# A delta-rule inverse with its first off-diagonal products written ahead of the diagonal blocks' copies, and filler steps dealt anew

## The chip, the cores and the metric

The kernel runs on one core of a Trainium2 chip. The metric is the device time of one execution in microseconds (us). The engines are PE (TensorE), DVE (VectorE), ACT (ScalarE), POOL (GpSimd) and SP (SyncE, which issues most DMAs).

## What is computed

Two layers (DEPTH = 2) work on 512 latent tokens and 256 context tokens of width 1024. Each layer has one input projection for three head groups, whose outputs are concatenated and projected again:

```python
h_l, h_c = rglru_bidir(a_l, a_c, ...)                 # gated linear recurrence, two directions
nb_l = neighbourhood_attend(q, k, v, kb_c, vb_c, rpb) # 6 heads, windows on an 8 x 64 grid
o_l, o_c = gdn_bidir(...)                             # gated delta rule, 4 heads, chunks of 64
y_l = concatenate([h_l * silu(za), nb_l * silu(zn), gdn_output(o_l, nw, zg)], -1) @ w_out
x_new = layer_norm(ALPHA * x + gate * y_l, ln_g, ln_b)
```

The change is in the third group. For each chunk of 64 tokens the delta rule solves a unit lower triangular system:

```python
a_mat = where(strict, einsum('nbhid,nbhjd->nbhij', kb, kc) * decay, 0.0) + eye(64)
u = triangular_solve(a_mat, vc * beta, lower=True, unit_diagonal=True)
w = triangular_solve(a_mat, kb * exp(gcum), lower=True, unit_diagonal=True)
```

There are 12 chunks (8 latent, 4 context), 4 heads and 2 directions. The kernel inverts each 64 x 64 matrix as two 32 x 32 diagonal blocks and one off-diagonal block, which is a product of three 32 x 32 matrices.

## The kernel before, in words

In each layer a generator `gdn()` gives the delta rule in 48 steps, and a generator `fill()` gives the rest: the attention's projections (`na_proj`, matmuls `pj<-uh,wh` and the like at L489, 24 for an output block of 512 or 256 columns), its scores and outputs (`na_att`), and the recurrence. A loop takes one step of `gdn()`, then as many steps of `fill()` as the table `CFG["n"][l]` says for that step, and calls a modulation gate at the steps of `CFG["mods"][l]`. The steps are: gates 0 and 1, chunk sets `cs` 2 to 7, transposes `t` 8 to 13, the decay products `w8` 14 to 19, two steps `lnT` 20 and 21, ten elimination steps `k3` to `k30` 22 to 31, `tz` 32, the inverse 33 to 35, and 12 scan steps from 36. A scheduler then sets the order on each engine, from this order of writing and from priorities; each engine's queue is run in order. `together` gives matmuls a high priority behind the first of them.

The parts that matter, for one layer:

- The matrices of the chunks lie in `bm`. Its diagonal blocks go into `dgc`, in a layout in which one partition row is one element of the block: two copies on ACT (L738) and two on DVE (L740), each 32 partitions by 1536. DVE transposes `dgc` to `ln` (L744).
- Elimination on DVE: 30 pairs of a product into `tmp` (L750) and a sum into `ln` (L752).
- DVE transposes `ln` into `tz` (L758, L759), the left factors of the off-diagonal products. It then transposes `ln` in place for d = 0 and d = 1, the two directions (L763), and ACT copies the blocks back into `bm`, four copies of 32 x 768 for each d (L767). The d = 0 copies read `ln` with a stride.
- Then two groups follow one another. Each has 48 products `gab<-tz,bm` (L779), an ACT copy to `zs` (L781), 48 products `gab<-bm,zs` (L788) and four DVE copies into `bm` (L794). All use the two banks of `gab`, one for the first products and one for the second.
- The scan's first ACT copies are `sb<-vtm` (L835). `dgc`, `ln`, `tz`, `so` and `sb` share two buffers (tag "g8"), so `sb` takes the buffer that `ln` had.

The attention's tiles that the profile names are `kT` and `qT` (ACT L924, DVE L925), `vT` (ACT L922), its transposes `nT` (PE L932) and their copies `vt` (ACT L933), scores `nS`, exponentials `nsb` (L980), `ptb` (L986), the product `nT<-ptb,vt` (PE L198, where the helper `mm` stands), and a weight's high and low part `wh` (ACT L237) and `wl` (DVE L238).

Of the kernel before, what the change touches and what calls it, by code (L numbers as in the profile page):

```python
# [5 lines left out]
F32 = mybir.dt.float32  # L6
# [50 lines left out]
ZXB = 5  # L57
CFG = {"gp": 3000, "sp": 2000, "mixP": 0.5, "wo": 1, "ye": 2, "rgord": [[0, 1, 0, 0, 0, 1, 0, 2, 1, 1, 2, 2, 2, 1, 2], [0, 0, 1, 0, 1, 0, 0, 2, 1, 1, 2, 1, 2, 2, 2]], "n": [[0, 0, 0, 0, 0, 0, 0, 0, 0, 2, 0, 3, 0, 0, 0, 0, 1, 2, 2, 0, 0, 1, 1, 0, 1, 0, 2, 0, 2, 0, 0, 0, 1, 0, 0, 0, 1, 1, 2, 0, 0, 2, 1, 0, 4, 0, 0, 0], [0, 0, 0, 0, 0, 0, 0, 0, 0, 1, 0, 0, 1, 0, 0, 0, 1, 2, 0, 1, 3, 0, 0, 1, 2, 0, 2, 0, 0, 0, 0, 0, 1, 0, 0, 2, 0, 0, 0, 3, 0, 0, 0, 0, 1, 0, 2, 2]], "mods": [[3, 5, 6, 8, 10, 11], [2, 11]]}

# [80 lines left out]
def _build(tc, I, out, dbg=None):  # L140
# [22 lines left out]
    def ps(tag, shape=(128, 512), dt=F32):  # L163
        return pp.tile(list(shape), dt, name=tag, tag=tag, bufs=PB[tag])
# [32 lines left out]
    def mm(o, a, b, start, stop):  # L197
        return lambda: T.matmul(o, a, b, start=start, stop=stop)  # L198
# [271 lines left out]
    for l in range(DEPTH):  # L470
# [99 lines left out]
        def gdn():  # L570
# [190 lines left out]
            yield  # L761
            for d in range(2):
                V.transpose(out=lview(d), in_=lview(d))  # L763
                for q in range(4):
                    c0 = 32 * (q % 2)
                    pr = slice(32 * q, 32 * q + 32)
                    S.activation(bm[pr, 24 * d:24 * d + 24, c0:c0 + 32],  # L767
                                 lview(d)[pr, :, 0:24].rearrange("p i m -> p m i"), AF.Copy)
            yield
            for mg_ in range(2):  # L770
                m0 = 12 * mg_
                zs = gp.tile([128, 512], F32, name="zs2", tag="qk", bufs=3)[:, 0:384].rearrange("p (m j) -> p m j", j=32)
# [167 lines left out]
        def na_att(hp):  # L940
            qT, kT, vt, z = nas[hp]
            for part in range(1 if last else 2):
                nq = 4 if part == 0 else 2
                nk = 4 if part == 0 else 2
                mx = np_.tile([128, 3, 4, 2], F32, name="mx", tag="mx", bufs=2)
                for b in range(nq):
                    p_ = ps("nS", TWO)
                    q0 = 128 * b + (0 if part == 0 else 512)
                    if part == 0 and b != 2:
                        sl = nbl[0] % 2  # L950
                        nbl[0] += 1
                        dma(out=bt[:, 2 * sl:2 * sl + 2], in_=I["rpb"][l, 2 * hp:2 * hp + 2, NA_KIND[b]].rearrange("h p k -> p h k"))
                    todo = []
                    for i, (a, c) in enumerate(((0, 0), (0, 1), (1, 0))):
                        for h2 in range(2):
# [14 lines left out]
                    for h2 in range(2):  # L970
# [12 lines left out]
                        for g in range(nk):  # L983
# [282 lines left out]
```

## Time and profile before

| | us |
|---|---|
| three runs | 893.71, 895.1, 898.94 |
| median | 895.1 |
| profiled execution | 896.31 |
| its span | 894.5 |
| PE busy in the span | 830.9 |
| DVE busy | 673.5 |
| ACT busy | 460.4 |
| POOL busy | 28.5 |

The span goes from the first to the last instruction of the profiled execution. The mean granted clock of PE over the span is 0.981 of full speed.

### The profile page before, as it was taken

Reading aid. Unit: us, or ns where it says so; the run is one execution under the profiler, and the core shown is the slowest. Engines: PE = TensorE matmul, PEld = TensorE weight load, DVE = VectorE, ACT = ScalarE, POOL = GpSimd, SP = SyncE. Lnnn points to the kernel's source line nnn. Section 1 sums busy time; section 2 is a strip of 40 time slices with the busy share of each in tenths; the row PEclk is TensorE's granted clock in tenths of the full one; section 3 lists DMA queues with packets and bytes.
Section 4 is the critical chain, followed back from the end, with each engine's and each line's share of the span. In section 5 each row is a group of like instructions: output and inputs, shape, how many; then the busy total and the mean of one; then the engine's idle time right before and its main releaser. Section 6 shows DMA issues by size and latency. Waiting matters only on the chain.

```text
span 894.5 us, 17977 instructions
## 1 busy us (share of the span) xinstructions
PE 830.9 (93%) x7164; PEld 634.6 (71%) x7164; DVE 673.5 (75%) x1524; ACT 460.4 (51%) x842; POOL 28.5 (3%) x101
## 2 busy tenths in 40 slices
PE   5999999998997999999999999999899699999885
PEld 3677777776776777877778778776777567776674
DVE  3458565897994699669969656998899467878867
ACT  3354443446457244489817634445554735349812
POOL 0000000000000011100001000000000000020001
PEclk8999999999999999999999999999899899999998
DMA  8826732211112010236533262121122121131433
GB/s 318 327 77 220 265 132 99 60 48 43 54 53 66 26 37 3 101 128 200 181 117 138 94 225 72 48 71 41 52 76 69 39 60 51 49 119 59 158 133 122
DMA packets 44900, 94.58 MB, mean 106 GB/s; under 512 B 5248, under 2 KB 10240, under 8 KB 44816
## 3 DMA queue, kind: packets, MB, share of 16 engines
q1 hardware_dynamic: 44816, 93.43, 31.2%
q8 instruction: 56, 0.92, 0.4%
q14 instruction: 28, 0.23, 0.1%
HBM read 84.22 MB, written 9.19 MB: 104 GB/s over the span
## 4 chain that ended last, share of the span: by engine, by line
PE 49%; DVE 26%; ACT 14%; issue 7%; DMA 3%; POOL 1%; SPq 1%; DVEq 0%; POOLq 0%; ACTq 0%
PE pj L489 23%; PE pj L1207 3%; DVE nsb L976 2%; DVE wl L238 2%; PE nT L984 2%; ACT bm L767 2%; DVE ln L752 2%; DVE tmp L750 2%; PE x L853 1%; PE x L1207 1%; PE nT L198 1%; PE x L198 1%; DVE ti L1085 1%; PE nS L590 1%; ACT wh L237 1%
## 5 line engine op out<-in xcount | busy, mean ns | idle before, releaser
L489 PE MATMUL pj<-uh,wh 128*128 128x512 f32 (+1 forms) x680 | 245.8, 362 | 0.8 <-ACT vT L922 0.8
L489 PE MATMUL pj<-uh,wl 128*128 128x512 f32 (+1 forms) x680 | 241.9, 356 | 0.0
L489 PE MATMUL pj<-ul,wh 128*128 128x512 f32 (+1 forms) x680 | 241.8, 356 | 0.0
L489 PEld LDWEIGHTS pj<-uh,wh 128*128 128x128 f32 x680 | 129.8, 191 | 22.7 <-issue 6.2
L489 PEld LDWEIGHTS pj<-ul,wh 128*128 128x128 f32 x680 | 129.7, 191 | 16.1 <-issue 2.5
L489 PEld LDWEIGHTS pj<-uh,wl 128*128 128x128 f32 x680 | 129.6, 191 | 16.0 <-issue 2.5
L238 DVE TENSOR_TENSOR wl<-raw,wh 128x512 fp32r<-128x512 f32 (+1 forms) x106 | 72.0, 681 | 48.6 <-ACT wh L237 47.1
L237 ACT ACTIVATE wh<-raw 128x512 fp32r<-128x512 f32 (+1 forms) x106 | 65.6, 622 | 63.8 <-PE pj L489 59.7
L980 ACT ACTIVATE nsb<-nsb,mx 128x512 f32<-128x512 f32 x48 | 34.5, 720 | 36.2 <-DVE mx L978 35.9
L986 ACT ACTIVATE ptb<-nT 128x512 f32<-128x512 f32 (+1 forms) x60 | 33.4, 556 | 23.8 <-PE nT L984 23.2
L984 PE MATMUL nT<-cst,nsb 128*128 128x128 f32 x216 | 36.8, 284 | 2.2 <-DVE mx L978 1.0
L543 DVE SCALAR_TENSOR_TENSOR cs<-xp,tph,cs 128x771 f32<-128x771 f32 (+1 forms) x36 | 35.0, 972 | 3.1 <-ACT cs L541 2.5
L198 PE MATMUL nT<-ptb,vt 128*64 128x128 f32 x432 | 31.1, 285 | 5.3 <-ACT ptb L986 5.3
L835 ACT ACTIVATE sb<-vtm 64x256 f32<-64x256 f32 x48 | 19.8, 413 | 27.8 <-DVE sb L846 20.8
L984 PEld LDWEIGHTS nT<-cst,nsb 128*128 128x128 f32 x216 | 23.4, 141 | 15.0 <-ACT nsb L980 5.1
L198 PEld LDWEIGHTS nT<-ptb,vt 128*64 128x64 f32 x432 | 23.7, 140 | 12.2 <-ACT ptb L986 11.2
L752 DVE TENSOR_TENSOR ln<-ln,tmp 128x60 f32<-128x60 f32 (+14 forms) x60 | 30.1, 502 | 1.2
L750 DVE TENSOR_TENSOR tmp<-ln 128x60 f32<-128x60 f32 (+14 forms) x60 | 30.1, 501 | 1.1
L198 PE MATMUL nS<-kT,qT 64*128 64x512 f32 (+1 forms) x180 | 27.6, 412 | 2.0 <-DVE mx L976 1.9
L1220 ACT ACTIVATE lsq<-rr,mv 128x1024 bf16<-128x1024 f32 x10 | 11.7, 1165 | 32.3 <-DVE mv L1218 32.3
L976 DVE CUSTOM_DVE_ANT_1 nsb<-nS,bt 128x512 f32<-128x512 f32 x36 | 24.3, 684 | 4.0 <-ACT ptb L986 1.4
L550 DVE SCALAR_TENSOR_TENSOR zs<-zs,pj 128x512 f32<-128x512 f32 (+1 forms) x24 | 14.0, 592 | 16.1 <-ACT zs L549 16.1
(299 smaller groups left out, 1676.8 us busy)
## 6 DMA issues: line engine op xcount, KB each, us to landing
raw<-in_win SPq DMA_DIRECT2D x104, 256.0 KB, 2.6
wm<-in_wmod SPq DMA_DIRECT2D x48, 512.0 KB, 6.6
raw<-in_wout SPq DMA_DIRECT2D x32, 256.0 KB, 2.7
bt<-in_rpb SPq DMA_DIRECT2D x18, 256.0 KB, 2.7
xt<-in_x SPq DMA_DIRECT2D x12, 256.0 KB, 7.8
xr<-in_x SPq DMA_DIRECT2D x12, 256.0 KB, 2.9
xpd<-xo SPq DMA_DIRECT2D x12, 256.0 KB, 2.1
yd<-zs SPq DMA_DIRECT2D x6, 384.0 KB, 3.0
```

The costliest lines, as they stand in the source:

```text
L198: return lambda: T.matmul(o, a, b, start=start, stop=stop)
L237: S.activation(h[:, :n], t[:, :n], AF.Copy)
L238: V.tensor_tensor(out=l[:, :n], in0=t[:, :n], in1=h[:, :n].bitcast(F32), op=ALU.subtract)
L489: T.matmul(q[:, :n], a[:, sl], b[:, bl_, kc, :], start=k == 0, stop=k == 23)
L543: V.scalar_tensor_tensor(o, x[:, lo_ + k:k + NCONV], taps[:, k:k + 1], o, op0=ALU.mult, op1=ALU.add)
L750: V.tensor_tensor(out=tv, in0=ln[:, :, k + 1:32, k:k + 1].to_broadcast([128, 2, n, k]), in1=ln[:, :, k:k + 1, 0:k].to_broadcast([128, 2, n ...
L752: V.tensor_tensor(out=ln[:, :, k + 1:32, 0:k], in0=ln[:, :, k + 1:32, 0:k], in1=tv, op=ALU.add)
L976: V.tensor_tensor_reduce(sb.rearrange("p (a b) -> p a b", a=2), p_[:, h2].rearrange("p (a b) -> p a b", a=2), bias, 1.0, -3e38, op0=ALU.ad ...
L980: S.activation(sb[:, 0:128 * nk], src, AF.Exp, bias=mx[:, 0, b, h2:h2 + 1], accum_out=mx[:, 1, b, h2:h2 + 1])
L984: T.transpose(pt[:, g, :], sb[:, 128 * g:128 * g + 128], ident)
L986: S.activation(t_[:, 0:nk], pt[:, 0:nk], AF.Copy)
L1207: T.matmul(q, a[:, t, kc, :], b, start=k == 0, stop=k == 23)
```

## The change

In the inverse, the first products of both groups are now written ahead of the copies, one group in each bank of `gab`, through `together`, each followed by its ACT copy `zs`. Then come the transposes of `ln`, d = 1 first; the four d = 1 copies stay on ACT and the four d = 0 copies go to DVE. The second products go to the same bank as their first ones. The number of steps is the same. Line numbers behind it fall by 7 or 8 (the products stand at L198, `zs` at L769, the transposes at L772, the copies at L778 and L780, the last copies at L787, `sb` at L828, `vT` at L915, `kT` at L917 and L918, `vt` at L926, `ptb` at L987).

The tables deal the same sums over other steps. In layer 0 the counts change at `w8_0` (0 to 1), `w8_3` and `w8_4` (2 to 1), the second `lnT` and `k3` (1 to 2), `k9` and `tz` (1 to 0) and `k24` (0 to 1); in layer 1 at `t3` (0 to 1), `t4` (1 to 0), `tz` (1 to 2) and the eleventh scan step (2 to 1), and the second gate moves from step 11 to step 7. The other new tables (`wos`, `yes`, `pv`) hold the old constants, and the regrouping in `na_att` does nothing with `pv` at 0.

```diff
-CFG = {"gp": 3000, "sp": 2000, "mixP": 0.5, "wo": 1, "ye": 2, "rgord": [[0, 1, 0, 0, 0, 1, 0, 2, 1, 1, 2, 2, 2, 1, 2], [0, 0, 1, 0, 1, 0, 0, 2, 1, 1, 2, 1, 2, 2, 2]], "n": [[0, 0, 0, 0, 0, 0, 0, 0, 0, 2, 0, 3, 0, 0, 0, 0, 1, 2, 2, 0, 0, 1, 1, 0, 1, 0, 2, 0, 2, 0, 0, 0, 1, 0, 0, 0, 1, 1, 2, 0, 0, 2, 1, 0, 4, 0, 0, 0], [0, 0, 0, 0, 0, 0, 0, 0, 0, 1, 0, 0, 1, 0, 0, 0, 1, 2, 0, 1, 3, 0, 0, 1, 2, 0, 2, 0, 0, 0, 0, 0, 1, 0, 0, 2, 0, 0, 0, 3, 0, 0, 0, 0, 1, 0, 2, 2]], "mods": [[3, 5, 6, 8, 10, 11], [2, 11]]}
+CFG = {"gp": 3000, "sp": 2000, "mixP": 0.5, "wo": 1, "ye": 2, "rgord": [[0, 1, 0, 0, 0, 1, 0, 2, 1, 1, 2, 2, 2, 1, 2], [0, 0, 1, 0, 1, 0, 0, 2, 1, 1, 2, 1, 2, 2, 2]], "n": [[0, 0, 0, 0, 0, 0, 0, 0, 0, 2, 0, 3, 0, 0, 1, 0, 1, 1, 1, 0, 0, 2, 2, 0, 0, 0, 2, 0, 2, 1, 0, 0, 0, 0, 0, 0, 1, 1, 2, 0, 0, 2, 1, 0, 4, 0, 0, 0], [0, 0, 0, 0, 0, 0, 0, 0, 0, 1, 0, 1, 0, 0, 0, 0, 1, 2, 0, 1, 3, 0, 0, 1, 2, 0, 2, 0, 0, 0, 0, 0, 2, 0, 0, 2, 0, 0, 0, 3, 0, 0, 0, 0, 1, 0, 1, 2]], "mods": [[3, 5, 6, 8, 10, 11], [2, 7]], "wos": [[1, 1, 1, 1, 1, 1, 1, 1, 1, 1, 1, 1, 1, 1, 1, 1, 1, 1, 1, 1], [1, 1, 1, 1, 1, 1, 1, 1, 1, 1, 1, 1, 1, 1, 1, 1, 1, 1, 1, 1]], "yes": [[2, 2, 2, 2, 2, 2, 2, 2, 2, 2, 2, 2, 2, 2, 2, 2, 2, 2, 2, 2], [2, 2, 2, 2, 2, 2, 2, 2, 2, 2, 2, 2, 2, 2, 2, 2, 2, 2, 2, 2]], "pv": [0, 0]}
@@ -759,40 +759,33 @@
             V.transpose(out=tz[:, 1].rearrange("p (m r) -> p r m", r=32), in_=ln[:, 1])
             tt3 = tz.rearrange("p d (m c) -> p d m c", c=32)
             yield
-            for d in range(2):
+            pz = [gt[:, g, 0:384].rearrange("p (m i) -> p m i", i=32) for g in range(2)]
+            offd = [(64 * hf + 32 * so, 64 * hf + 32 * (1 - so), d, so) for hf in range(2) for d, so in ((0, 1), (1, 0))]
+            zs = []
+            for g in range(2):
+                together(mm(pz[g][b:b + 32, m, :], bm[a:a + 32, 24 * d + 12 * g + m, 32 * so:32 * so + 32],
+                            tt3[a:a + 32, d, 12 * g + m, :], True, True) for m in range(12) for b, a, d, so in offd)
+                zs.append(gp.tile([128, 512], F32, name="zs2", tag="qk", bufs=3)[:, 0:384].rearrange("p (m j) -> p m j", j=32))
+                S.activation(zs[g], pz[g], AF.Copy)
+            yield
+            for d in (1, 0):
                 V.transpose(out=lview(d), in_=lview(d))
                 for q in range(4):
                     c0 = 32 * (q % 2)
                     pr = slice(32 * q, 32 * q + 32)
-                    S.activation(bm[pr, 24 * d:24 * d + 24, c0:c0 + 32],
-                                 lview(d)[pr, :, 0:24].rearrange("p i m -> p m i"), AF.Copy)
-            yield
-            for mg_ in range(2):
-                m0 = 12 * mg_
-                zs = gp.tile([128, 512], F32, name="zs2", tag="qk", bufs=3)[:, 0:384].rearrange("p (m j) -> p m j", j=32)
-                pz = gt[:, 0, 0:384].rearrange("p (m i) -> p m i", i=32)
-                for m in range(12):
-                    for hf in range(2):
-                        for d in range(2):
-                            si, so = (0, 1) if d == 0 else (1, 0)
-                            a, b = 64 * hf + 32 * si, 64 * hf + 32 * so
-                            T.matmul(pz[b:b + 32, m, :], bm[a:a + 32, 24 * d + m0 + m, 32 * so:32 * so + 32],
-                                     tt3[a:a + 32, d, m0 + m, :], start=True, stop=True)
-                S.activation(zs, pz, AF.Copy)
-                pr_ = gt[:, 1, 0:384].rearrange("p (m i) -> p m i", i=32)
-                for m in range(12):
-                    for hf in range(2):
-                        for d in range(2):
-                            si, so = (0, 1) if d == 0 else (1, 0)
-                            a, b = 64 * hf + 32 * si, 64 * hf + 32 * so
-                            T.matmul(pr_[a:a + 32, m, :], zs[b:b + 32, m, :],
-                                     bm[b:b + 32, 24 * d + m0 + m, 32 * so:32 * so + 32], start=True, stop=True)
-                for hf in range(2):
-                    for d in range(2):
-                        si, so = (0, 1) if d == 0 else (1, 0)
-                        a = 64 * hf + 32 * si
-                        V.tensor_copy(bm[a:a + 32, 24 * d + m0:24 * d + m0 + 12, 32 * so:32 * so + 32], pr_[a:a + 32])
-                yield
+                    dst, src = bm[pr, 24 * d:24 * d + 24, c0:c0 + 32], lview(d)[pr, :, 0:24].rearrange("p i m -> p m i")
+                    if d:
+                        S.activation(dst, src, AF.Copy)
+                    else:
+                        V.tensor_copy(dst, src)
+            yield
+            for g in range(2):
+                together(mm(pz[g][a:a + 32, m, :], zs[g][b:b + 32, m, :],
+                            bm[b:b + 32, 24 * d + 12 * g + m, 32 * so:32 * so + 32], True, True)
+                         for m in range(12) for b, a, d, so in offd)
+                for b, a, d, so in offd:
+                    V.tensor_copy(bm[a:a + 32, 24 * d + 12 * g:24 * d + 12 * g + 12, 32 * so:32 * so + 32], pz[g][a:a + 32])
+            yield
 
             for z_ in Z:
                 next(z_, 0)
```

Three places of the order, as the scheduler gives it. First ACT in layer 1, from the attention's last `kT` of its pair of heads to `vt`, before:

```order
L924 ACTIVATE kT<-pj 128x256
L922 ACTIVATE vT<-pj 128x8x64
L237 ACTIVATE wh<-raw 128x512
L767 ACTIVATE bm<-ln 32x24x32 x2
L237 ACTIVATE wh<-raw 128x512
L922 ACTIVATE vT<-pj 128x256
L767 ACTIVATE bm<-ln 32x24x32 x5
L237 ACTIVATE wh<-raw 128x512
L767 ACTIVATE bm<-ln 32x24x32
L781 ACTIVATE zs_7500<-gab 128x384
L835 ACTIVATE sb<-vtm 64x256 x4
L933 ACTIVATE vt<-nT 128x512 x2
```

And after the change:

```order
L917 ACTIVATE kT<-pj 128x256
L778 ACTIVATE bm<-ln 32x24x32 x2
L915 ACTIVATE vT<-pj 128x8x64
L778 ACTIVATE bm<-ln 32x24x32
L237 ACTIVATE wh<-raw 128x512
L778 ACTIVATE bm<-ln 32x24x32
L828 ACTIVATE sb<-vtm 64x256
L237 ACTIVATE wh<-raw 128x512
L828 ACTIVATE sb<-vtm 64x256 x3
L915 ACTIVATE vT<-pj 128x256
L926 ACTIVATE vt<-nT 128x512 x2
L237 ACTIVATE wh<-raw 128x512
```

The first two copies into `bm` moved ahead of the first `vT`, the four `sb` moved ahead of the `vT` of 256 and of `vt`, and four copies and the first `zs` are gone from this stretch.

DVE at the same place, from the last steps of the elimination to the transposes of `ln`, before:

```order
L750 TENSOR_TENSOR tmp<-ln 128x168
L925 SCALAR_TENSOR_TENSOR kT<-pj,kT 128x256
L752 TENSOR_TENSOR ln<-ln,tmp 128x2x3x28
L750 TENSOR_TENSOR tmp<-ln 128x116
L756 MEMSET ln 128x2x32
L752 TENSOR_TENSOR ln<-ln,tmp 128x2x2x29
L750 TENSOR_TENSOR tmp<-ln 128x60
L752 TENSOR_TENSOR ln<-ln,tmp 128x2x30
L758 STREAM_TRANSPOSE tz<-ln 128x32x32
L759 STREAM_TRANSPOSE tz<-ln 128x32x32
L763 STREAM_TRANSPOSE ln<-ln 128x1024
L763 STREAM_TRANSPOSE ln<-ln 128x32x32
```

And after:

```order
L750 TENSOR_TENSOR tmp<-ln 128x60
L1014 TENSOR_TENSOR zs<-zs,nT 128x512
L752 TENSOR_TENSOR ln<-ln,tmp 128x2x30
L758 STREAM_TRANSPOSE tz<-ln 128x32x32
L238 TENSOR_TENSOR wl<-raw,wh 128x512 x2
L759 STREAM_TRANSPOSE tz<-ln 128x32x32
L918 SCALAR_TENSOR_TENSOR kT<-pj,kT 128x256
L772 STREAM_TRANSPOSE ln<-ln 128x32x32
L772 STREAM_TRANSPOSE ln<-ln 128x1024
L780 COPY bm<-ln 32x24x32 x4
L238 TENSOR_TENSOR wl<-raw,wh 128x512 x4
```

The `kT` of 256 columns moved from the elimination to behind the last transpose into `tz`, the transpose of the view 32x32 (d = 1) moved ahead of the other, and four copies into `bm` follow.

PE in layer 1 at the first products, which stood behind the 24 projections of 256 columns, before:

```order
L489 MATMUL pj<-uh,wl 128x256
L779 MATMUL gab<-tz,bm 32x32 x48
L932 MATMUL nT<-cst,vT 128x128 x4
L489 MATMUL pj<-uh,wh 128x512
L489 MATMUL pj<-ul,wh 128x512
L489 MATMUL pj<-uh,wl 128x512
```

And after, where they stand behind the next 24 projections (of 512 columns) and the transposes of `vT`, whose last projection is the first row:

```order
L489 MATMUL pj<-uh,wl 128x512
L198 MATMUL gab<-tz,bm 32x32 x48
L198 MATMUL nS<-kT,qT 128x512 x6
L198 MATMUL gab<-tz,bm 32x32 x48
L489 MATMUL pj<-uh,wh 128x512
L198 MATMUL nS<-kT,qT 128x512 x6
L198 MATMUL gab<-bm,zs_7594 32x32 x48
L985 MATMUL nT<-cst,nsb 128x128 x4
L489 MATMUL pj<-ul,wh 128x512
L489 MATMUL pj<-uh,wl 128x512
L846 MATMUL x<-sb,bm 64x64
L489 MATMUL pj<-uh,wh 128x512
```

Both groups of first products and twelve score products now stand ahead of the first group of second products.

Last, ACT in layer 0 at the copies into `dgc`, before:

```order
L986 ACTIVATE ptb<-nT 128x256
L738 ACTIVATE dgc<-bm 32x2x24x32
L986 ACTIVATE ptb<-nT 128x256
L738 ACTIVATE dgc<-bm 32x2x24x32
L922 ACTIVATE vT<-pj 128x8x64
L237 ACTIVATE wh<-raw 128x512 x2
L922 ACTIVATE vT<-pj 128x256
L933 ACTIVATE vt<-nT 128x512 x2
```

And after:

```order
L987 ACTIVATE ptb<-nT 128x256
L738 ACTIVATE dgc<-bm 32x2x24x32 x2
L237 ACTIVATE wh<-raw 128x512
L987 ACTIVATE ptb<-nT 128x256
L915 ACTIVATE vT<-pj 128x8x64
L237 ACTIVATE wh<-raw 128x512
L915 ACTIVATE vT<-pj 128x256
L926 ACTIVATE vt<-nT 128x512 x2
```

The second `ptb` of this place moved behind the second copy into `dgc` and a `wh`.

## Rows read from the trace of the kernel before

**Rows 1.** The page, part 1: busy time, share of the span and instructions.
```profile
PE 830.9 (93%) x7164; PEld 634.6 (71%) x7164; DVE 673.5 (75%) x1524; ACT 460.4 (51%) x842; POOL 28.5 (3%) x101
```

**Rows 2.** Waits of PE by line and releaser: sum, times, longest (us).
```profile
PE pj L1171 <- ACT uh L1043: 7.3, 4, 3.1
```

**Rows 3.** Timeline of PE, layer 0: start, length, operation, tiles, count, [idle before <- releaser].
```profile
211.36 0.66 PE L198 MATMUL nT<-ptb,vt 128*64 128x128 f32 x8 [1.30 <-ACT ptb L986]
...
215.48 0.50 PE L489 MATMUL pj<-uh,wh 128*128 128x512 f32 x1 [0.79 <-ACT vT L922]
...
217.28 0.63 PE L932 MATMUL nT<-cst,vT 128*128 128x128 f32 x4 [0.84 <-DVE zs L1009]
...
276.25 0.66 PE L932 MATMUL nT<-cst,vT 128*128 128x128 f32 x4 [1.67 <-ACT vt L933]
...
278.51 0.33 PE L932 MATMUL nT<-cst,vT 128*128 128x128 f32 x1 [0.67 <-ACT vt L933]
...
288.03 1.02 PE L788 MATMUL gab<-bm,zs 32*32 32x32 f32 x96 [1.49 <-ACT zs L781]
```

**Rows 4.** Timeline of PE, layer 1.
```profile
639.34 1.97 PE L198 MATMUL nT<-ptb,vt 128*64 128x128 f32 x16 [3.00 <-ACT ptb L986]
...
693.83 0.39 PE L489 MATMUL pj<-uh,wl 128*128 128x512 f32 x1
694.06 0.28 PE L489 MATMUL pj<-uh,wh 128*128 128x256 f32 x1
694.17 0.28 PE L489 MATMUL pj<-ul,wh 128*128 128x256 f32 x1
...
710.53 1.50 PE L788 MATMUL gab<-bm,zs 32*32 32x32 f32 x96 [6.56 <-ACT zs L781]
...
712.88 1.11 PE L932 MATMUL nT<-cst,vT 128*128 128x128 f32 x4 [0.85 <-ACT vt L933]
```

**Rows 5.** Windows: length, then PE, PEld, DVE, ACT, POOL busy (instructions), granted clock, DMA.
```profile
639.30:645.50 6.20, 6.16 (x34) 5.64 (x35) 4.73 (x6) 2.64 (x4) 0.00 (x0) 0.50 0.15 42
708.00:717.00 9.00, 5.62 (x112) 3.98 (x112) 3.96 (x7) 6.37 (x12) 0.00 (x0) 0.50 0.11 31
831.00:834.00 3.00, 2.41 (x10) 1.99 (x11) 2.25 (x4) 1.85 (x5) 0.00 (x0) 1.00 0.84 293
...
645.50:697.10 51.60, 50.65 (x326) 39.59 (x324) 49.30 (x109) 23.52 (x43) 0.16 (x3) 1.00 0.24 72
```

**Rows 6.** Timeline of ACT, layer 1, the inverse.
```profile
698.38 3.48 ACT L767 ACTIVATE bm<-ln 32x768 f32<-32x768 f32 x2 [2.18 <-DVE ln L763]
...
709.12 0.84 ACT L767 ACTIVATE bm<-ln 32x768 f32<-32x768 f32 x1
...
710.50 1.71 ACT L835 ACTIVATE sb<-vtm 64x256 f32<-64x256 f32 x4
712.23 0.60 ACT L933 ACTIVATE vt<-nT 128x512 f32<-128x512 f32 x1
```

**Rows 7.** Timeline of DVE, layer 1, elimination and inverse.
```profile
645.26 0.69 DVE L238 TENSOR_TENSOR wl<-raw,wh 128x512 fp32r<-128x512 f32 x1 [1.15 <-ACT kT L924]
...
691.32 0.42 DVE L925 SCALAR_TENSOR_TENSOR kT<-pj,kT 128x256 fp32r<-128x256 f32 x1
...
695.28 2.02 DVE L759 STREAM_TRANSPOSE tz<-ln 128x1024 f32<-128x1024 f32 x1
697.16 3.40 DVE L763 STREAM_TRANSPOSE ln<-ln 128x1024 f32<-128x1024 f32 x2
```

**Rows 8.** Groups by shape: line, engine, operation, count | busy, mean ns | idle before.
```profile
L738 ACT ACTIVATE dgc<-bm 32x1536 f32<-32x1536 f32 x4 | 11.7, 2933 | 0.4 <-DVE bm L725 0.4
...
L740 DVE COPY dgc<-bm 32x1536 f32<-32x1536 f32 x4 | 7.0, 1738 | 0.1
```

**Rows 9.** Timeline of DVE, layer 0: the two transposes of the inverse.
```profile
270.25 1.25 DVE L763 STREAM_TRANSPOSE ln<-ln 128x1024 f32<-128x1024 f32 x1
...
272.29 2.23 DVE L763 STREAM_TRANSPOSE ln<-ln 128x1024 f32<-128x1024 f32 x1
```

More of the change, by code (lines that the diff above doesn't have):

```diff
@@ L945, in na_att, with scores @@
                 mx = np_.tile([128, 3, 4, 2], F32, name="mx", tag="mx", bufs=2)
-                for b in range(nq):
+                def scores(b):
                     p_ = ps("nS", TWO)
+                    sl = (nbl[0] - (b == 2)) % 2
                     q0 = 128 * b + (0 if part == 0 else 512)
                     if part == 0 and b != 2:
-                        sl = nbl[0] % 2
                         nbl[0] += 1
@@ L964, in na_att @@
                             todo.append(mm(po_, qT[a][pr, q0:q0 + 128], kb, i == 0, i == 2))
-                    together(todo)
+                    return p_, sl if part == 0 else 0, todo
+                sl = 0
+                nxt = None
+                for b in range(nq):
+                    p_, sl, todo = nxt or scores(b)
+                    if not nxt:
+                        together(todo)
+                    nxt = None
                     if part == 1:
@@ L989, in na_att @@
                     po = ps("nT")[:, 0:128]
-                    together(mm(po[64 * h2:64 * h2 + 64, :], vt[:, vs[g], 64 * h2:64 * h2 + 64], ptb[h2][:, g, :],
-                                g == 0, g == nk - 1) for g in range(nk) for h2 in (1, 0))
+                    todo = [mm(po[64 * h2:64 * h2 + 64, :], vt[:, vs[g], 64 * h2:64 * h2 + 64], ptb[h2][:, g, :],
+                               g == 0, g == nk - 1) for g in range(nk) for h2 in (1, 0)]
+                    if b < nq - 1 and CFG["pv"][l]:
+                        nxt = scores(b + 1)
+                        todo = todo + nxt[2] if CFG["pv"][l] == 1 else nxt[2] + todo
+                    together(todo)
                     if part == 0:
@@ L1151, in _build @@
             raise ValueError("order")
-        for _ in f:
-            wo_load(CFG["wo"])
+        for step, _ in enumerate(f):
+            wo_load(CFG["wos"][l][step])
             if len(zdone) == 3:
-                for u in early[:CFG["ye"]]:
+                ye = CFG["yes"][l][step]
+                for u in early[:ye]:
                     if u not in ydone:
                         y_load(u)
-                del early[:CFG["ye"]]
+                del early[:ye]
         wo_load(16)
```

## The prediction

> **What bounds the kernel now.** I read the page's busy shares first: PE is busy 830.9 us of a span of 894.5, DVE 673.5, ACT 460.4 [rows 1]. PE is the bound as a whole, so what a change of order can win is PE's idle time, about 64 us, and what slow clock follows it. Next I read where PE waits around the code that is edited, from the timeline of PE. In layer 0 there are two clusters: after the copies into `dgc` 1.30, 0.79 and 0.84 us, and in the inverse 1.67, 0.67 and 1.49 us [rows 3]. In layer 1 there is one of 3.00 us after `dgc`, and in the inverse the longest of the kernel, 6.56 us, with 0.85 us behind it [rows 4]. Last I read the clock. [...] A stall of 3.1 us later in the kernel [rows 2] was followed by a clock of 1.00 [rows 5], so stalls of about 3 us go either way.
>
> The reader is also to see that the two layers differ. In layer 1, DVE is busy 49.30 of the 51.60 us from the elimination to its transposes into `tz` [rows 5]: that stretch runs at DVE's pace, and `tz` ends at 697.3 [rows 7]. In layer 0, `tz` is done by 270.25, where the next transpose starts [rows 9], and PE still has most of 18 us of other work ahead of the second products at 288.03 [rows 3].
>
> **The change part by part.** *Layer 1, the inverse.* Before, ACT makes all eight copies of the diagonal blocks ahead of `zs`. The two first take 3.48 us, so a d=0 copy is 1.74; a d=1 copy is 0.84 [rows 6]. The 6.56 us are the wait for that row of copies. The change takes the four d=0 copies off ACT, and PE gets 24 projections and nine transposes ahead of the products. But the order shows two new places in line. ACT's `vT` now stands behind two d=1 copies, and these wait for DVE's transpose of d=1. ACT's `sb`, ahead of `vt`, reuses the buffer of `ln` (tag g8, two buffers), so it waits for the four d=0 copies now on DVE; `vt` is what PE's second set of transposes waits for.
>
> I count from D, the end of DVE's `kT` of 256, which was at 691.7 [rows 7] and now comes behind L759. PE's 24 projections of 256 columns wait for it and start 0.11 to 0.12 us apart [rows 4]: D+2.9. DVE's d=1 transpose is 2.23 us [rows 9], ACT's two copies 1.7, `vT` as a copy of 512 like `vt` 0.60 [rows 6]: D+4.5. So PE waits 1.6. Then four transposes (0.4, an estimate from 1.11 at half clock with a little overlap, [rows 4]) and ten projections at 0.23 (the distance of the first two such rows, [rows 4]): D+7.2. Meanwhile DVE does the d=0 transpose, 3.40 less 2.23, 1.2 [rows 7, 9], and four copies. An ordinary DVE copy of a `bm` layout, twice the size, is 1.738 us, against 2.933 on ACT [rows 8]; half of it is 0.87, four are 3.5: D+6.9. [...] I take 0.87, as the pattern of L740 is the nearest. Then on ACT four `sb` 1.71, a `wh` and a short `vT` (about 1.0 by the 0.60 of 512 elements), `vt` 0.60 [rows 6]: D+10.2. PE waits 3.0. With 0 to 0.8 us for `kT` itself (I take 0.4) the stretch has 5.0 us of stalls where it had 6.56 and 0.85: **-2.4 us**. The two banks do not overlap: in the order the second group of first products waits for the first group's `zs`, but six score products cover that.
>
> [...]
>
> *Layer 0, the inverse.* The first two copies on ACT come after 2.23 us of transpose [rows 9] and take 1.7, against 1.2 and 3.5: 0.7 us earlier, so the wait of 1.67 becomes 1.0. The copy ahead of the next `vt` is 0.84, not 1.7, so 0.67 goes. ACT has about 6.9 us less to do ahead of the first `zs`, so the 1.49 goes. DVE has the four copies, 3.5 us, in the stretch of 18 us in which PE works on its other projections, so they cost nothing; without that cover they would cost their 3.5. **-2.8 us.**
>
> *The redealt steps, layer 0.* The order has `dgc`, `dgc`, `wh`, `ptb` where `ptb` stood between the two copies. `ptb` is late by one 2.93 copy [rows 8] and a `wh` of 0.6, 3.5 us. PE has sixteen more projections of 256 ahead of its wait, 1.9 us. So 1.30 becomes 2.9. `vT`, next in line, is then 0.5 late, not 0.79, and the 0.84 has time to go. 2.93 becomes 3.4: **+0.5 us**.
>
> *The redealt steps, layer 1.* Six score products and fifteen projections stand ahead of the transposes that wait for `ptb` behind `dgc`, where two sets of transposes and 24 projections stood; each sums to 4.8 to 4.9 us. The 3.00 becomes 3.2: **+0.2 us**. One block of attention, some 3.6 us of PE, moves from ahead of `dgc` to behind it, so that DVE's elimination starts as much earlier; this is why D cannot be compared in absolute time. The earlier gate in layer 1 (7 for 11) and its loads move by a few steps in a stretch where PE does not wait; I cost it nothing, and if its weights came late it would cost a load's rest.
>
> *The clock.* The fall at the 6.56 us goes, -2.8. New pieces of 2.9 (layer 0) and 3.0 (layer 1) are of the size that did and didn't bring a fall; I let one of the two, +2.8. The one after layer 1's `dgc` stays.
>
> The sum is 0.5 - 2.8 + 0.2 - 2.4 - 2.8 + 2.8 = -4.5 us. It is made against the profiled execution, 896.3 us, of which 894.5 is the span and 1.8 lies around it. That execution is 1.2 us over the median of 895.1. So the forecast is 891.8 less 1.2, **890.6 us**. About 0.5%, 4.5 us here, is what a measurement of this kernel can tell from no change, so this lies right on that edge.
>
> **The rivals.** *Both new stalls or neither bring a fall.* For: 3.00 did; against: 3.1 did not. Both: 893.4; neither: 887.8.
>
> [...]
>
> *The stall is only moved.* DVE's copies cost ACT's 1.74: 3.5 us more, 894.1, and `vt` stalls PE 6.5 us in one piece. For it: the same strided read cost ACT twice a d=1 copy.
>
> *Slower: holes in the elimination.* In layer 1, DVE's elimination now holds nine blocks of score work and six of output; before, a few such handoffs waited, the longest 1.15 us [rows 7], 2.3 us in all [rows 5]. As the stretch runs at DVE's pace, each hole is paid in full. Were eleven more to wait, at 1.15, it would be +12.7, 903.3; it is slower than the bound of 899.6 from 0.82 us each. Against it: PE is ahead of DVE there and has its scores ready.
>
> **How the numbers follow.** One fall 0.35; neither 0.20; both 0.13; stall gone 0.14; only moved 0.08; holes 0.10. Half of the first lies under 890.6. Faster by over 0.5%: 0.17 + 0.20 + 0.14 and a little of the rest, 0.53. Slower: 0.09, the greater part of the holes. Same: 0.38. The range of 882 to 898 takes in the bounds of the copies and of the clock and all cases but the holes. The first case's own range is 888.5 to 893.
>
> **What would show it.** The L780 copies: 0.87 each. Layer 1: PE waits of about 1.6 for `vT` and 3.0 for `vt`, none of over 1 for `zs`. Layer 0: a wait of about 2.9 at the product with `ptb`, and in the inverse one of 1.0. The granted clock after each of these decides among the cases. I am wrong if `vt` does not wait for `sb` on ACT, if DVE's elimination takes other than some 51 us, or if PE's order is not what fills the time.

## The result

The changed kernel takes 886.13 us, median of four runs (885.2 to 888.96), beside 896.21 us for the kernel before (893.71 to 898.94). The ratio is 0.9896, with a 95% interval from 0.9867 to 0.9926. Run again beside other kernels on one chip it was 886.15, with a ratio of 0.9894 (0.9875 to 0.9913). The forecast was 890.6 with a range of 882 to 898: the sign and the range held, and the gain came out at 9 to 10 us where 4.5 were forecast. One execution of one of the kernels below took 4327.67 us at a mean granted clock of 0.168 and is left out of its median and its ratio.

The page of the profiled execution after the change, its span and busy times:

```profile
span 884.5 us, 17982 instructions
...
PE 829.5 (94%) x7164; PEld 634.2 (72%) x7164; DVE 680.8 (77%) x1532; ACT 446.7 (51%) x834; POOL 28.9 (3%) x101
```

PE's busy time hardly moved (830.9 before, [rows 1]), and the span is 10 us shorter, so most of it is idle time of PE, 63.6 us before and 55.0 now. The timeline of PE shows where it waits (start, length, operation, count, and in brackets the idle time before it with its releaser):

```profile
216.02 0.66 PE L198 MATMUL nT<-ptb,vt 128*64 128x128 f32 x8 [3.06 <-ACT ptb L987]
...
273.93 0.63 PE L925 MATMUL nT<-cst,vT 128*128 128x128 f32 x4 [0.36 <-DVE zs L1014]
...
276.71 0.66 PE L925 MATMUL nT<-cst,vT 128*128 128x128 f32 x4 [0.53 <-ACT vt L926]
...
288.27 0.80 PE L198 MATMUL gab<-bm,zs 32*32 32x32 f32 x71
290.52 0.39 PE L198 MATMUL gab<-bm,zs 32*32 32x32 f32 x25 [1.44 <-issue]
...
634.13 1.11 PE L985 MATMUL nT<-cst,nsb 128*128 128x128 f32 x4 [3.48 <-ACT ptb L987]
...
697.43 0.66 PE L925 MATMUL nT<-cst,vT 128*128 128x128 f32 x4 [1.35 <-ACT vT L915]
...
702.73 0.66 PE L925 MATMUL nT<-cst,vT 128*128 128x128 f32 x4 [2.34 <-ACT vt L926]
...
711.28 0.90 PE L198 MATMUL gab<-bm,zs 32*32 32x32 f32 x84 [0.32 <-ACT zs L769]
```

These answer to [rows 3, 4]. In layer 0 the three pieces after `dgc` (1.30, 0.79, 0.84) are one of 3.06. In its inverse 1.67, 0.67 and 1.49 are 0.36 and 0.53, but a new piece of 1.44 stands in the middle of the second products, which the profile calls "issue": PE waits for nothing that it shows. In layer 1, 3.00 after `dgc` is 3.48, and in the inverse 6.56 and 0.85 are 1.35, 2.34 and 0.32. The timelines of ACT and DVE in layer 1's inverse say why, and answer to [rows 6, 7]:

```profile
694.55 1.70 ACT L778 ACTIVATE bm<-ln 32x768 f32<-32x768 f32 x2 [5.97 <-DVE ln L772]
696.27 1.11 ACT L915 ACTIVATE vT<-pj 128x512 f32<-128x512 f32 x1
697.40 0.84 ACT L778 ACTIVATE bm<-ln 32x768 f32<-32x768 f32 x1
698.27 0.63 ACT L237 ACTIVATE wh<-raw 128x512 fp32r<-128x512 f32 x1
698.93 0.84 ACT L778 ACTIVATE bm<-ln 32x768 f32<-32x768 f32 x1
699.80 0.42 ACT L828 ACTIVATE sb<-vtm 64x256 f32<-64x256 f32 x1
700.13 0.61 ACT L237 ACTIVATE wh<-raw 128x512 fp32r<-128x512 f32 x1
700.76 1.16 ACT L828 ACTIVATE sb<-vtm 64x256 f32<-64x256 f32 x3
701.83 0.36 ACT L915 ACTIVATE vT<-pj 128x256 f32<-128x256 f32 x1
702.09 0.58 ACT L926 ACTIVATE vt<-nT 128x512 f32<-128x512 f32 x1
```

```profile
690.06 2.08 DVE L759 STREAM_TRANSPOSE tz<-ln 128x1024 f32<-128x1024 f32 x1
692.00 0.40 DVE L918 SCALAR_TENSOR_TENSOR kT<-pj,kT 128x256 fp32r<-128x256 f32 x1
692.33 3.28 DVE L772 STREAM_TRANSPOSE ln<-ln 128x1024 f32<-128x1024 f32 x2
695.65 3.44 DVE L780 COPY bm<-ln 32x768 f32<-32x768 f32 x4
```

DVE ends `tz` at 692.1, then does `kT`, both transposes (3.28 us together) and the four d = 0 copies, 3.44 us, 0.86 each. ACT's first d = 1 copies start at 694.55, with the end of the first of these transposes, and `vT` ends behind them. From there to 702.67 ACT has no pause. `sb` starts at 699.80, when ACT's own last copy has ended (699.77); DVE's last d = 0 copy had ended 0.7 us earlier (699.09), so what `vt` stands behind is ACT's own row of work and not the buffer that `sb` takes over. `vt` ends at 702.67, when PE's second set of transposes starts.

The clock, in windows (length; PE, PEld, DVE, ACT and POOL busy; granted clock; DMA):

```profile
217.00:220.00 3.00, 3.00 (x9) 2.43 (x9) 2.97 (x5) 0.90 (x2) 0.00 (x0) 0.50 0.28 87
634.00:640.00 6.00, 5.87 (x33) 5.31 (x34) 5.05 (x9) 2.51 (x6) 0.00 (x0) 0.50 0.15 46
697.00:700.00 3.00, 2.57 (x14) 2.19 (x14) 2.76 (x4) 2.90 (x5) 0.00 (x0) 1.00 0.00 0
703.00:706.00 3.00, 3.00 (x17) 2.42 (x16) 0.69 (x1) 1.32 (x3) 0.00 (x0) 1.00 0.15 59
```

It falls to 0.50 after both stalls behind a `dgc`, and not in layer 1's inverse, where it had been at 0.50 over nine microseconds [rows 5].

### The profile page after: what moved, and what is told of

Its sections match the earlier page's. It is cut to its first block, busy times and chain, and to the rows that moved or that the text cites. A ratio compares the mean times of both kernels' runs of the same rounds, so it can differ in the third digit from the quotient of the medians.

```text
span 884.5 us, 17982 instructions
## 1 busy us (share of the span) xinstructions
PE 829.5 (94%) x7164; PEld 634.2 (72%) x7164; DVE 680.8 (77%) x1532; ACT 446.7 (51%) x834; POOL 28.9 (3%) x101
## 4 chain that ended last, share of the span: by engine, by line
PE 56%; DVE 22%; ACT 10%; issue 6%; DMA 3%; POOL 1%; SPq 1%; DVEq 0%; POOLq 0%; ACTq 0%
PE pj L489 26%; PE pj L1213 3%; PE nT L985 2%; PE nT L198 2%; DVE wl L238 2%; PE x L846 2%; DVE nsb L977 2%; PE x L198 1%; PE x L1213 1%; PE gab L198 1%; PE nS L198 1%; DVE ti L1090 1%; PE nS L590 1%; ACT wh L237 1%; ACT dgc L738 1%
## 5 line engine op out<-in xcount | busy, mean ns | idle before, releaser
L987 ACT ACTIVATE ptb<-nT 128x512 f32<-128x512 f32 (+1 forms) x60 | 33.4, 557 | 26.0 <-PE nT L985 25.5
L198 PE MATMUL nT<-ptb,vt 128*64 128x128 f32 x432 | 31.1, 285 | 3.4 <-ACT ptb L987 3.4
L828 ACT ACTIVATE sb<-vtm 64x256 f32<-64x256 f32 x48 | 19.6, 413 | 23.7 <-DVE sb L839 14.0
L198 PEld LDWEIGHTS nT<-ptb,vt 128*64 128x64 f32 x432 | 23.7, 140 | 10.2 <-ACT ptb L987 9.3
L198 PE MATMUL nS<-kT,qT 64*128 64x512 f32 (+1 forms) x180 | 26.9, 403 | 1.0 <-DVE mx L977 0.9
L539 ACT ACTIVATE xp<-pj 128x512 f32<-128x512 f32 (+1 forms) x30 | 14.7, 488 | 21.8 <-PE pj L489 18.0
```

The source lines that it names most:

```text
L987: S.activation(t_[:, 0:nk], pt[:, 0:nk], AF.Copy)
```

## Experiments

Two theories stood against each other. A: the gain of the inverse comes from dealing the copies to two engines, and most of it lies in layer 1. B: it comes from the tables, which move projections to where PE would wait. A rival to A is C: what counts is that the products are written ahead of the copies. Ratios are against the kernel before on the same chip, with 95% intervals.

**The inverse alone**: both lists of `"n"` as in the kernel before, and the old `"mods"` (`[...]` stands for the lists).

```diff
-CFG = {... "n": [[...], [...]], "mods": [[3, 5, 6, 8, 10, 11], [2, 7]], ...}
+CFG = {... "n": [[...], [...]], "mods": [[3, 5, 6, 8, 10, 11], [2, 11]], ...}
```

> The new inverse with the old tables. Theory A (the inverse's code removes the stall of layer 1 and the stalls of layer 0's inverse, the tables add one 3 us stall in layer 0 and little else): 7 to 10 us under the kernel before, no wait of over 3 us for zs in layer 1, and the stall after dgc in layer 0 back at 1.3 us. Theory B (the tables make the gain, by moving projections to where PE would wait): within 3 us of the kernel before, a wait of 5 us or more left in layer 1's inverse.

Measured: 889.29 us, ratio 0.9933 (0.9904 to 0.9962), 6 us under the kernel before, a little short of what A gave. Its ten executions go from 885.62 to 894.17 us, the five over 891 at a mean granted clock of 0.981 or less and the others above that; the profiled one is the shortest of them. PE's timeline:

```profile
210.49 0.66 PE L198 MATMUL nT<-ptb,vt 128*64 128x128 f32 x8 [1.29 <-ACT ptb L987]
...
699.14 1.50 PE L198 MATMUL gab<-tz,bm 32*32 32x32 f32 x96 [3.81 <-ACT zs L769]
```

The stall after layer 0's `dgc` is back at its first length, as A said. Layer 1 has its wait for `zs` still, at 3.81 us where 6.56 stood, so A's "none of over 3 us" did not hold: with the old tables the first products come before the projections again, and ACT's copies are fewer, not gone.

**The tables alone**, with the old inverse: the same lists, the other way round, in the kernel before.

> The old inverse with the new tables. Theory A: within 3 us of the kernel before; layer 0 has the stall of 3.1 us after dgc, layer 1 a wait of 4 us or more for zs behind the eight copies on ACT. Theory B: 7 us or more under the kernel before.

Measured: 893.35 us, ratio 0.9969 (0.9948 to 0.9991), 2 to 3 us under the kernel before. PE's timeline:

```profile
289.30 1.02 PE L788 MATMUL gab<-bm,zs 32*32 32x32 f32 x96 [1.51 <-ACT zs L781]
...
699.79 0.66 PE L932 MATMUL nT<-cst,vT 128*128 128x128 f32 x4 [2.02 <-ACT vT L922]
...
705.73 1.12 PE L932 MATMUL nT<-cst,vT 128*128 128x128 f32 x4 [3.66 <-ACT vt L933]
```

So theory B falls: the tables give less than a third by themselves. The wait for `zs` in layer 1 is down to 0.35 us, but PE waits for `vT` and `vt` in its place, 5.7 us together and the second with a fall of the clock behind it; layer 0's 1.51 for `zs` stays.

**All copies on ACT**, the rest as changed:

```diff
-                    if d:
-                        S.activation(dst, src, AF.Copy)
-                    else:
-                        V.tensor_copy(dst, src)
+                    S.activation(dst, src, AF.Copy)
```

> The changed kernel with the four d=0 copies given back to ACT; the rest as changed. Theory A (the shared copies are part of the gain, since a d=0 copy is 1.74 us on ACT and 0.86 on DVE): 3 to 6 us over the changed kernel, with waits for zs or vt of 4 us or more in layer 1. Rival (writing the products ahead is all that matters, the copies lie under projections): within 2 us of the changed kernel.

Measured: 896.13 us, ratio 1.0001 (0.9984 to 1.0019). The whole gain is gone, 10 us where A had said 3 to 6. In layer 1 four waits of 1.0 to 2.9 us for ACT's `vT`, `vt` and `zs` stand where the changed kernel has three, none of 4 us as A had it, and the layer is 2.6 us longer. The surprise is layer 0, where the loss is 7 us from the first product of its decay steps to the start of its recurrence (213.6 us against 206.6). ACT there, then PE, then a window:

```profile
280.06 6.40 ACT L777 ACTIVATE bm<-ln 32x768 f32<-32x768 f32 x4
286.48 0.60 ACT L549 ACTIVATE zs<-pj 128x512 f32<-128x512 f32 x1
```

```profile
287.86 0.50 PE L489 MATMUL pj<-uh,wh 128*128 128x512 f32 x1 [1.79 <-DVE zs L550]
...
290.70 1.51 PE L198 MATMUL gab<-tz,bm 32*32 32x32 f32 x96 [1.78 <-ACT zs L769]
```

```profile
289.00:302.00 13.00, 10.94 (x221) 7.86 (x221) 3.58 (x7) 2.12 (x6) 0.00 (x0) 0.50 0.14 43
```

Four d = 0 copies take 6.40 us in one piece on ACT, 1.60 each. `zs` of the gate and then `zs` of the products stand behind them, PE waits twice 1.8 us, and the clock is at half for some 13 us. PE is busy 10.94 us of that window. In the changed kernel the projections of 512 columns start 0.43 us apart at 0.50 (at 217 us) and 0.23 at 1.00 (at 704 us). In that proportion, an estimate, 5 of the 7 us are the price of the clock and the waits are the smaller part. I had looked for the loss in layer 1 alone.

**The copies dealt out, the products not ahead.** The kernel before with the new tables and only this:

```diff
-            for d in range(2):
+            for d in (1, 0):
...
-                    S.activation(bm[...], lview(d)[...], AF.Copy)
+                    if d: S.activation(dst, src, AF.Copy)
+                    else: V.tensor_copy(dst, src)
```

> The new tables and the old order of writing (first products after the copies, second products in the other bank, groups one after the other), with the copies dealt as in the change: d=1 first, d=1 on ACT, d=0 on DVE. Theory A (the copies' split carries the gain of the inverse): within 2 us of the changed kernel, so 8 to 11 us under the kernel before. Theory C (the products written ahead carry it): 4 us or more over the changed kernel, with a wait for zs of 2 us or more in layer 1.

Measured: 886.05 us, ratio 0.9901 (0.9876 to 0.9926), the same as the changed kernel. PE's timeline in layer 1's inverse has the same two waits:

```profile
695.00 0.66 PE L935 MATMUL nT<-cst,vT 128*128 128x128 f32 x4 [1.34 <-ACT vT L925]
...
700.29 0.66 PE L935 MATMUL nT<-cst,vT 128*128 128x128 f32 x4 [2.35 <-ACT vt L936]
```

So C falls. With the new tables the four kernels make a square. The ratios are each against the kernel before on its own chip; the layers, from the first decay product to the recurrence, are those of the profiled executions, two of them for the changed kernel.

| | median | ratio | layer 0 | layer 1 |
|---|---|---|---|---|
| neither edit | 893.35 | 0.9969 | 208.8 | 192.6 |
| products ahead alone | 896.13 | 1.0001 | 213.6 | 190.3 |
| copies dealt alone | 886.05 | 0.9901 | 204.1 | 190.6 |
| both | 886.1 | 0.9896 | 206.6, 205.5 | 187.8, 186.7 |

Dealing the copies is the whole of the inverse's gain. By these executions most of it lies in layer 0 (4.7 and 7.0 us, against 2.0 and 2.6 in layer 1), the other way round from A; two executions of the changed kernel differ by 1.1 us in each layer. Writing the products ahead is not without effect, but its two effects about cancel: layer 1 gets 2 to 4 us shorter and layer 0 longer by 1.4 to 4.8. In all rows but the first the transpose of d = 1 also comes ahead of d = 0; that order by itself was not tried, and the step from the second row to the last, 10 us, does not contain it. Nor was the dealing tried alone with the old tables.

**Three copies into `dgc` on DVE, one on ACT**, the rest as changed:

```diff
-                if q < 2:
+                if q < 1:
                     S.activation(dst, src, AF.Copy)
```

> The changed kernel with three copies into dgc on DVE and one on ACT, where two and two stood. Theory A (what is left of PE's stalls comes from ptb standing behind 5.9 us of dgc copies on ACT, and each stall brings a fall of the clock): the stalls of 3.06 and 3.48 us fall under 1 us, the falls at both places go, 8 to 11 us under the changed kernel. Rival (the copies only move to DVE, which then starts the elimination later, and layer 1 is bound by DVE): 0 to 4 us under the changed kernel, with longer waits for vT and vt in layer 1's inverse.

Measured: 885.05 us, ratio 0.9885 (0.9846 to 0.9924), about 1 us under the changed kernel, within the error. PE's timeline:

```profile
211.85 0.66 PE L198 MATMUL nT<-ptb,vt 128*64 128x128 f32 x8 [1.28 <-ACT ptb L987]
...
219.08 0.41 PE L1010 MATMUL nT<-cst,rb 128*128 128x128 f32 x2 [1.36 <-DVE rb L1007]
...
629.65 0.66 PE L985 MATMUL nT<-cst,nsb 128*128 128x128 f32 x4 [1.72 <-ACT ptb L987]
...
634.65 0.66 PE L985 MATMUL nT<-cst,nsb 128*128 128x128 f32 x4 [0.79 <-ACT nsb L981]
...
693.51 0.66 PE L925 MATMUL nT<-cst,vT 128*128 128x128 f32 x4 [0.87 <-ACT vT L915]
...
699.64 0.66 PE L925 MATMUL nT<-cst,vT 128*128 128x128 f32 x4 [2.73 <-ACT vt L926]
```

The time went as the rival said. The stalls after `dgc` fell to 1.28 and 1.72, but 1.36 and 0.79 came behind them, for DVE's `rb` and for ACT's `nsb`, and layer 1's inverse still waits 0.87 and 2.73, 3.6 in all where the changed kernel has 3.7; that they would be longer did not come. The elimination starts 40.7 us after the layer's first decay product, where the two executions of the changed kernel have 41.5 and 40.9, and that stretch goes at DVE's pace. No fall of the clock followed the stalls after `dgc`, one of 3.4 us followed the 2.73.

**The first `sb` on GpSimd**, the rest as changed:

```diff
+                    if s < 2: G.tensor_copy(vst[...], vtm[...])
+                    else: S.activation(vst[...], vtm[...], AF.Copy)
-                    S.activation(vst[...], vtm[...], AF.Copy)
```

> The changed kernel with the copies sb of the first two scan steps on GpSimd, so that ACT's vt in layer 1 has nothing ahead of it that waits for DVE's d=0 copies. Theory A (the 2.34 us that PE waits for vt come from sb, which waits for those copies): that wait falls to 0.5 us or less and the kernel is 2 to 2.5 us under the changed one. Rival (GpSimd is slow at copies, and the scan's first products or DVE, whose buffer it shares, wait for sb instead): 0 to 3 us over the changed kernel.

Measured: 888.13 us, ratio 0.9930 (0.9908 to 0.9953). PE's two sets of transposes:

```profile
700.05 0.66 PE L928 MATMUL nT<-cst,vT 128*128 128x128 f32 x4 [1.34 <-ACT vT L918]
...
703.85 0.66 PE L928 MATMUL nT<-cst,vT 128*128 128x128 f32 x4 [2.21 <-ACT vt L929]
```

The wait for `vt` is 2.21 us, not 0.5, but the distance between the two sets of transposes is 3.8 us where it was 5.3. `vt` did come 1.5 us earlier; the scheduler put four projections there instead of ten, and six behind. So the 1.6 us of `sb` in ACT's queue were what it saved. Layer 1 as a whole took 186.5 us, 187.75 and 186.7 in the two executions of the changed kernel, so little of the difference can be put down to the edit. Layer 0 was 2 to 3 us longer, with 1.32 and 1.77 us of issue waits in its inverse. Neither theory had that, and GpSimd was not slow here: a copy of 64 x 256 took it 0.44 us and ACT 0.42.

**Layer 0's old counts**: the first list of `"n"` as in the kernel before, the rest as changed.

> The changed kernel with layer 0's old counts (layer 1's new ones and the new gate step are kept). Theory A (the tables' gain is layer 1's alone; in layer 0 they bring a stall of 3.06 us in one piece with a fall of the clock for three pieces of 2.9 us in all without one): 0 to 3 us under the changed kernel. Theory B (layer 0's counts carry gain too): 2 us or more over the changed kernel.

Measured: 887.4 us median of four, ratio 0.9919 (0.9891 to 0.9946). This bears out neither A nor B: 1.3 us over the changed kernel by the medians, with intervals that overlap. The issue wait in layer 0 was 1.99 us with a fall of the clock behind it.

**Both of these edits:**

> Both of the two edits above: layer 0's old counts, and the first sb on GpSimd. Theory A: 2 to 5 us under the changed kernel, without a fall of the clock in layer 0 and without a wait for vt of over 0.5 us in layer 1. Rival: no different from the changed kernel within 2 us, since layer 1 then waits for DVE at the next place in line.

Measured: 887.95 us, ratio 0.9929 (0.9901 to 0.9956), within 2 us of the changed kernel, as the rival said. Neither sign of A came: a fall of the clock followed an issue wait of 1.72 us in layer 0, and the wait for `vt` in layer 1 was 2.21.

**A version by layers.** Since layer 0 was shortest with the old order of writing (204.1 us in the kernel with the copies dealt alone, 206.6 in the changed one), and layer 1 with the new order and `sb` on GpSimd, I put these together. In layer 0 the transposes and dealt copies come first and then the groups one after the other, as in the kernel before; layer 1 is as changed. In the second, layer 0's `dgc` has three copies on DVE as well.

```diff
+            if l == 0:
+                for d in (1, 0):
+                    V.transpose(out=lview(d), in_=lview(d))
...
+                        if d: S.activation(dst, src, AF.Copy)
+                        else: V.tensor_copy(dst, src)
+                for g in range(2):
...
+                    S.activation(zt, pz[0], AF.Copy)
...
+            else:
...
+                    if s < 2 and l == 1: G.tensor_copy(vst[...], vtm[...])
```

> The changed kernel itself, beside the two below on one chip: 8 to 11 us under the kernel before, with the same waits as in its first trace.

> The copies dealt as in the change in both layers, layer 0 with the products in the old order of writing, layer 1 in the new one and with its first sb on GpSimd. Theory D (in layer 0, three groups of 96 small matmuls close together bring the wait that the profile calls issue, 1.4 us in the changed kernel, and the old order keeps them apart; in layer 1 the changed order and sb on GpSimd gain 1 us): 2.5 to 4 us under the changed kernel, no wait of over 0.5 us called issue in layer 0. Rival (these differences between layers were chance, as issue falls elsewhere from run to run): within 1.5 us of the changed kernel, the issue wait appears at another group.

> The kernel above with layer 0's copies into dgc one on ACT and three on DVE. Theory D: the stall of 3.0 us in layer 0 becomes two of about 1.3 us without a fall of the clock, 1 to 3 us under the kernel above. Rival (layer 0's later work then waits for DVE): within 1 us of it.

Measured, on one chip: the changed kernel 886.15 us, 0.9894 (0.9875 to 0.9913); the version by layers 884.14, 0.9873 (0.9853 to 0.9893); with `dgc` three to one in layer 0, 883.38, 0.9857 (0.9833 to 0.9881). The changed kernel came again as expected. The version by layers is 2.0 us under it by the medians, between D's 2.5 to 4 and the rival's 1.5, so the two are not told apart. The last is the fastest here, 2.8 us under the changed kernel; the intervals of the ratios still overlap, but all four of its executions (881.87 to 884.13) lie under all four of the changed kernel (885.95 to 886.61). Against the version by layers it is 0.8 us shorter, within the rival's 1 us, though the stall of 3.0 became two of 1.3 as D had it. Layer 0 of the version by layers had one issue wait, of 0.54 us, at another group:

```profile
295.49 0.50 PE L786 MATMUL gab<-bm,zs 32*32 32x32 f32 x35 [0.54 <-issue]
```

In the last one the two stalls after `dgc`, 1.28 us for `ptb` and 1.31 for DVE's `rb`, were not followed by a fall of the clock.

## Why the forecast was right in its sign and short in its size

*The waits of layer 1's inverse.* The order of events counted from D came as forecast; the lengths in it did not all. The d = 0 copies took 0.86 us (0.87 forecast, from half of L740), and `vT` and `vt` came behind what the order showed. But PE began its 24 projections 0.66 us after D, so that it was ready for its two sets of transposes at D+3.7 and D+8.0 where 2.9 and 7.2 were counted. `vT` took 1.11 us where 0.60 was counted and ended at D+5.0, `vt` at D+10.3. So PE waited 1.35 and 2.34 us (1.6 and 3.0 forecast): errors of up to 0.8 us that partly cancel. Nothing was lost for `kT`. The link from the d = 0 copies to `vt` through the buffer of `sb` was not the one that held, as ACT was busy with its own copies until after them. That the copies' split is what pays is shown by the square above. The 0.86 us for 768 elements is 1.12 ns an element, beside the 1.13 of L740 [rows 8]. The range took in copies at half of 0.87 us; no run shows one, and the eight of L780 in the two layers took 0.83 to 0.88.

*Layer 0.* After `dgc`, 2.9 was forecast and 3.06 measured, and nothing behind it where I had 0.5. In the inverse the waits that were forecast came out right in sum (1.0 in all, 0.9 measured, of which 0.36 is for DVE's `zs` and not for ACT), and with the copies dealt alone the 2.8 came in full: 3.83 us of waits became 0.93. But the issue wait of 1.44 us, which came with the products written ahead, took back half of it. I had no such term; [rows 3] have no such wait of that size in layer 0's inverse. Nor had I a term for two waits of the kernel before that the redealt steps took away:

```profile
230.23 0.96 PE L198 MATMUL nS<-kT,qT 64*128 64x512 f32 x6 [0.89 <-DVE mx L976]
...
239.24 0.98 PE L198 MATMUL nT<-ptb,vt 128*64 128x128 f32 x14 [0.49 <-ACT ptb L986]
```

Neither is in the changed kernel, and with the old tables (the inverse alone) they are back, 0.89 and 0.51. PE's idle time in layer 0 outside the two clusters fell from 6.7 to 4.9 us.

*The sum, term by term*, from the two profiled executions:

| | forecast | measured |
|---|---|---|
| layer 0, after `dgc` | +0.5 | +0.1 |
| layer 0, inverse | -2.8 | -1.5 |
| layer 1, after `dgc` | +0.2 | +0.5 |
| layer 1, inverse | -2.4 | -3.4 |
| the clock in layer 1's inverse and at new stalls | 0.0 | -1.1 (estimate) |
| sum | -4.5 | -5.4 |

Single terms are off by up to 1.3 us either way, and nearly cancel. So the forecast is not short because of a term that it has: the two spans differ by 10.0 us, and 4.6 of these lie where it counted nothing.

*The clock.* The 2.8 is half of the 5.62 us in which PE was busy at 0.50 [rows 5]. No run shows this price: in the changed kernel the 0.43 us from one projection of 512 columns to the next at 0.50 are 0.23 at 1.00, and a group of 96 small matmuls took 1.50 us at 0.50 [rows 4] and 1.02 at 1.00. "I let one of the two, +2.8": one did come in the profiled execution, in layer 0, but it lasted 3.4 us, 1.7 by the same half, and none came in layer 1's inverse, so that by this estimate 1.1 of the 2.8 of the old fall was gained where the sum had nothing. The same program shows how little can be forecast here. In the second profiled execution of the changed kernel the stall in layer 0 was 3.02 us, and no fall followed; after the 3.47 us of layer 1 the clock was low for 3.4 us, where it was low for 6.8 in the first:

```profile
216.00:219.00 3.00, 2.77 (x14) 2.02 (x13) 2.99 (x5) 1.05 (x3) 0.00 (x0) 1.00 0.25 87
633.00:638.00 5.00, 4.91 (x37) 4.28 (x36) 4.65 (x9) 2.42 (x5) 0.00 (x0) 0.66 0.20 52
```

*What is not settled.* By pieces of the two profiled executions, the stretch up to layer 0's first decay product became 1.2 us longer, layer 0 (to its recurrence) 1.9 shorter, the stretch between the layers 2.0, layer 1 5.5 and the tail 1.9; in the second execution of the changed kernel layer 0 gave 3.0 and layer 1 6.5. The tail has the same order of PE in all 13 profiled executions and takes from 97.3 to 101.0 us, 98.8 and 101.0 in the two of the changed kernel, so its 1.9 can be chance. In the stretch between, the order changes with the second gate's new step. With the old order it took 217.6 us in the kernel before and 216.2 with the inverse alone, so 1.3 of the 2.0 can be chance too. What is left of this part stays open.

Of the rivals, "only moved" fell with the price of the copies. "Holes in the elimination" fell with DVE's pace: it was busy 50.6 of the 52.8 us from the first product of the elimination to the end of `tz`, 48.2 of 50.5 before. "Stall gone" did not come either: 4.0 us are left of layer 1's 7.4.

## What to carry to other kernels

Where an engine's queue of copies keeps a bound engine waiting, measure the copy on both engines with the stride that it has: here the same read cost 1.6 to 1.74 us on ScalarE and 0.86 on VectorE, and moving four of them was the whole gain of the inverse, part of it a fall of the clock that did not come. Writing the consumers earlier gave nothing in sum, as it won in one layer what it lost in the other: read such an edit by layers. Count the new waits from the order before the run, one queue after the other from the last common event; here they came out within a microsecond. Count them also where only the order moves and no code is edited, as what this forecast missed lay there. Give a fall of the clock a range and not a price.

## What the runs showed of the hardware that was not expected

*Where the waits called "issue" end.* Groups of 96 small matmuls (32 x 32), each with its weight load, took 1.02 us each in the changed kernel at a clock of 1.00, one of them 1.28. In layer 0, where the changed order has three of them close together, PE stopped in the third for 1.32 to 1.99 us with nothing to wait for in the profile; in the two executions of the changed kernel it was 1.44 and 1.43 us at the same matmul. Three groups close together are not enough for it, for in layer 1 of the same execution two of them stand as close, with the third at 711.28 (above), and PE stopped in none:

```profile
706.67 1.02 PE L198 MATMUL gab<-tz,bm 32*32 32x32 f32 x96
708.51 1.02 PE L198 MATMUL gab<-tz,bm 32*32 32x32 f32 x96
```

The traces show a DMA queue that they name "instruction", with 56 packets of 16 KB in the execution:

```profile
q8 instruction: 56, 0.92, 0.4%
```

PE has 14,328 matmuls and weight loads, and in the changed kernel 69 semaphore and drain instructions with them. Over the 13 profiled executions it has 15 waits of more than 0.15 us called "issue", and each ends 1.2 to 1.6 us after a packet of this queue has landed. The kernel before has two of them, 0.18 us at 296.28 and 0.21 at 721.34, and the changed kernel the one at 290.52: they end 1.42, 1.24 and 1.47 us after a packet. If all these instructions of PE are numbered in order from 0, the three end at 4,545, 11,458 and 4,289. The first is 256 above the third, and the second is 27 times 256 and 1 above the first. What the packets hold, and whether PE waits for one, is not shown. In layer 0 of the changed kernel the 256 matmuls and weight loads ahead of the stop took 2.29 us:

```profile
286.79:289.08 2.29, 2.28 (x128) 1.74 (x128) 0.00 (x0) 0.49 (x1) 0.00 (x0) 1.00 0.39 114
```

In layer 1 the two runs of 256 that follow the first group took 3.8 and 4.4 us, with other work between the groups. No run moved a group by some instructions while all else stayed, so the cause of the waits is not shown, nor how much work between the groups is enough.

*The clock after a stall.* A stall of 3.0 to 3.5 us behind layer 1's `dgc` was followed by a fall to 0.50 in all 12 executions that had one. One of 3.0 to 3.1 us behind layer 0's `dgc` was followed by a fall in 4 of 7, and of the two executions of the changed kernel in one. A stall of 3.12 us at 831.59 in the kernel before was followed by none, the same one of 3.13 at 823.55 in the changed kernel by a fall. The falls inside the two layers lasted from 3.4 to 13.6 us, the longest behind two stalls of 1.8 us.
